# Spreading the root of each head's mean square: a stride-zero stationary and one product per head in place of a wide tile and transposes

## The chip, the core and the metric

The kernel runs on one core of a Trainium2 chip. The metric is the device time of one execution in microseconds (us). TensorE is PE in the profile (its weight loads are listed apart as PEld), VectorE is DVE, ScalarE is ACT, GpSimd is POOL, and SyncE, which issues the DMAs, is SP.

## What is computed

Two layers over 512 latent tokens and 256 context tokens, model width 1024. Layer 0 is grouped-query attention, layer 1 a bidirectional state-space mixer; each is followed by a gated FFN with a short convolution. What matters here is the normalization, which occurs in two shapes:

```python
def rms_norm(x, g):
    xf = x.astype(jnp.float32)
    y = xf * lax.rsqrt(jnp.mean(xf * xf, axis=-1, keepdims=True) + EPS)
    return (y * g.astype(jnp.float32)).astype(x.dtype)
...
    q_l = rms_norm(q_l.reshape(bsz, seq, N_HEADS, HEAD_DIM), q_norm)
    k_l = rms_norm(k_l.reshape(bsz, seq, N_KV_HEADS, HEAD_DIM), k_norm)
...
        h_l = modulate(rms_norm(x, norm_mix_w[i]), mod_l[0], mod_l[1])
```

Before every mixer and FFN the norm runs over the whole width of 1024 (one root per token). On queries and keys it runs per head of 64 (one root per token and head): 16 query heads and 4 key heads, 768 tokens each.

## The kernel before

All activations lie transposed: channels on the 128 partitions, tokens along the free dimension. A tile of queries or keys therefore holds two heads, one on partitions 0 to 63 and one on 64 to 127, and 768 tokens in six groups of 128. There are ten such tiles (eight of queries, two of keys).

The large matrix products run in fp32r, each as three products of a high and a low part (`mm3`, lines 103 to 111). Products whose operands are plain fp32 go through the same instruction. The trace counts how many records an instruction leaves, and this count will matter: a transpose leaves one, an fp32r product one, a plain fp32 product two.

The helper `rstd_rows` (lines 235 to 267) makes the roots. It is a generator in two halves with a `BREAK` between them:

1. Sums of squares. For each group of 128 tokens, the squared tile is the stationary operand and `cols` the moving one (line 244), so that a group's tokens come to lie on partitions and the result has `c` columns: `c` is 1 for the norm over the width and 2 for queries and keys (one column per head). DVE adds epsilon (line 247), ACT takes the logarithm and the exponential (line 249), DVE makes one Newton step (lines 251, 252 and its last multiply).
2. The way back. The root is on the token's partition, but it has to multiply a tile with tokens along the free dimension. So every group is transposed on PE into a PSUM bank, four groups to a bank, and the yielded bank is the second operand of a DVE multiply (line 552 for queries and keys, line 294 for the others).

For `c` = 1 the last Newton multiply writes the small tile `a` (128 x 6 at most) and the transpose reads one of its columns with a stride of zero 128 times. For `c` = 2 the last multiply writes a wide tile `rb` (128 x 768), in which every root stands 64 times (line 259, tile `rbq` in the trace), and the transpose reads 128 columns of it.

Where it is called:

- queries and keys, ten times, in `normed` (line 538), each with two yields of the second half: four groups (512 latent tokens), then two (256 context tokens). The first two calls (keys 0, queries 0) lie in the context projection (`ps_c`, line 719), where the scheduler has put their six transposes together. The next two (queries 1 and 2) lie in the value projection (`ps_v`, line 533). The other six lie in the steps of the head pairs, one in each of the first six pairs (line 789), where PE runs the scores (`ps_s`, line 697), the maxima (`ps_m`, line 625), the value products (`ps_o`, `ps_oc`, line 661), the sums (`ps_sum`, line 667) and pieces of the query projection (`ps_q`) in the order of the program. There the transposes follow right behind a group of `ps_o`.
- the width norm, six tiles of 128 tokens before attention (`rsTa`), ten in the two FFN norms (`rsTf`), six before the state-space layer (`rsTs`) and four at its gated norm (`rsTy`).

Up to line 515, the first projection, PE, ACT and DVE are ordered by hand; behind that a list scheduler orders instructions by the program's order and its own costs, so a changed instruction can move its neighbours. Tiles named `t3` come from a pool of 18 buffers in this stage; `rb` takes one of them.

Of the kernel before, what the change touches and what calls it, by code (L numbers as in the profile page):

```python
# [7 lines left out]
P = 128  # L8
# [3 lines left out]
ALU = mybir.AluOpType  # L12
# [55 lines left out]
def t3(g, name, dt=F32, n=T):  # L68
    return g.t3p.tile([P, n], dt, tag="t3", bufs=g.n3, name=name)
# [148 lines left out]
def follow(g, bi):  # L218

    if g.last_act is not None:  # L220
        g.tc.add_manual_dep(bi.ins, g.last_act.ins.name, mybir.DependencyInfo(
            mybir.DependencyClass.NoSync, mybir.DependencyReason.DATA), reason="order of tables")
    g.last_act = bi
# [11 lines left out]
def rstd_rows(g, sq, n, cols, width, name, bank):  # L235

    nc = g.nc
    c = cols.shape[-1]  # L240
    nt = n // P
    ps = bank(f"ss{name}")
    for t in range(nt):
        nc.tensor.matmul(ps[:, t * c : (t + 1) * c], sq[:, t * P : (t + 1) * P], cols, start=True, stop=True)
    small = lambda nm: g.p.tile([P, nt * c], F32, tag="rst", bufs=8, name=nm)
    a, y, u = small("rsa"), small("rsy"), small("rsu")
    nc.vector.tensor_scalar(a, ps[:, : nt * c], 1.0 / width, EPS, ALU.mult, ALU.add)

    for f in ((lambda: nc.scalar.activation(y, a, AF.Ln)), (lambda: nc.scalar.activation(y, y, AF.Exp, scale=-0.5))):
        follow(g, f()) if g.tables else f()  # L250
    nc.vector.tensor_tensor(u, y, a, ALU.mult)
    nc.vector.scalar_tensor_tensor(u, y, -0.5, u, ALU.mult, ALU.mult)
    if c == 1:
        nc.vector.scalar_tensor_tensor(a, u, 1.5, y, ALU.add, ALU.mult)
        root = lambda t: a[:, t : t + 1].broadcast_to([P, P])
    else:
        rb = t3(g, f"rb{name}", n=n)
        wide = lambda v: v.unsqueeze(2).broadcast_to([P, nt * c, P // c])
        nc.vector.scalar_tensor_tensor(rb.rearrange("p (a b) -> p a b", b=P // c), wide(u), 1.5, wide(y),
                                       ALU.add, ALU.mult)  # L260
        root = lambda t: rb[:, t * P : (t + 1) * P]
    yield BREAK
    for t0 in range(0, nt, 4):
        pt = bank(f"rsT{name}")
        for t in range(t0, min(nt, t0 + 4)):
            nc.tensor.transpose(pt[:, (t - t0) * P : (t - t0 + 1) * P], root(t), g.ident)
        yield (pt, t0 * P, min(n, (t0 + 4) * P))


# [53 lines left out]
class Norm:  # L323
# [23 lines left out]
    def gen(self, seg, x, lag=2):  # L347

        i, a, b = seg
        g, nc, n = self.g, self.g.nc, b - a  # L350
        for _ in range(lag):
            yield
        rows = rstd_rows(g, self.acc[seg, 6], n, g.ones[:, :1], D, self.name, lambda nm: Bank(g, nm))
        next(rows)
        for _ in range(lag):
            yield
        rs = next(rows)[0][:, :n]
        for m in range(KT):
            modulated(g, self.h[i][m], x[i], rs, a, b, *self.a, self.streams[i][1], m,
                      pool=m in ((1, 4) if a else (1, 3, 5, 7)))  # L360
            yield
# [30 lines left out]
def attention(g, fill, X, late):  # L392
# [57 lines left out]
    for m in range(KT):  # L450
        sq = t2("sql") if m else acc
        nc.scalar.activation(sq, xs[0][m], AF.Square)
        if m:
            nc.vector.tensor_tensor(acc, acc, sq, ALU.add)
    norm = rstd_rows(g, acc, L, g.ones[:, :1], D, "a", Bk)
    g.qn8 = g.const.tile([P, 1], F32, name="qn8")
    nc.vector.tensor_scalar(g.qn8, g.par[:, PC["qn"] : PC["qn"] + 1], HD ** -0.5, None, ALU.mult)
# [23 lines left out]
    for m in range(KT):  # L481
# [11 lines left out]
        if m == 3:  # L493
            norm = rstd_rows(g, sqc, C, g.ones[:, :1], D, "a", Bk)
            next(norm)
# [1034 lines left out]
```

## Time and profile before

| | |
|---|---|
| median of 3 runs | 1875.17 us (1874.18 to 1875.43) |
| profiled execution: its own time | 1875.38 us |
| profiled execution: span | 1873.6 us |
| mean granted PE clock | 0.998 |
| PE busy | 1848.9 us, 99% |
| DVE busy | 1303.6 us, 70% |
| ACT busy | 807.3 us, 43% |
| POOL busy | 299.8 us, 16% |

The time of an execution is 1.8 us above its span. A timeline row gives the start, the length, the engine, the line, the operation with its tiles (output, then inputs), the shape (stationary rows * columns, then the moving partitions x columns) and a count. A row of several records is merged: its length runs from the first start to the last end, so the spacing of n records of length d in a row of length T is (T - d) / (n - 1). Matmuls are pipelined, and their own lengths overlap; spacing and the start of the next row are what cost time. The bracket at a row's end is idle time of the engine before it and what ended that.

### The profile page before, as it was taken

The numbers are of one execution on the slowest core, as the hardware profiler recorded it, in microseconds if no ns is written. First come the engines' busy times: TensorE is split into PE (matmuls) and PEld (weight loads), VectorE is DVE, ScalarE is ACT, GpSimd is POOL, SyncE is SP. The second block draws the span as 40 slices with busy tenths as digits, with TensorE's granted clock in tenths as the row PEclk, the third lists the DMA queues.
The fourth block names the chain that finished last, engine by engine and source line by source line (L and its number), as shares of the span: only waits on it lengthen the run. The fifth ranks groups of instructions, "written<-read, shape, count | busy, mean of one in ns | idle before, by whom it ended". The sixth has DMA issues, their size and how long they took to land.

```text
span 1873.6 us, 28798 instructions
## 1 busy us (share of the span) xinstructions
PE 1848.9 (99%) x11474; PEld 1547.2 (83%) x11474; DVE 1303.6 (70%) x1950; ACT 807.3 (43%) x1402; POOL 299.8 (16%) x266
## 2 busy tenths in 40 slices
PE   9999999999999999999999999999999999999999
PEld 8876656798888888888888888888887888888887
DVE  6588888778787776544487787777797565565655
ACT  4534444363122222222367667776666352323231
POOL 2123120040000000000032333444443210000000
PEclk9999999999999999999999999999999999999999
DMA  9233151124444552211224432443352223222232
GB/s 345 76 109 101 63 178 52 57 84 164 146 135 145 191 185 99 68 58 56 68 91 141 124 105 87 124 124 113 124 178 93 79 91 97 95 95 97 90 103 89
DMA packets 74070, 211.67 MB, mean 113 GB/s; under 512 B 9040, under 2 KB 14544, under 8 KB 73808
## 3 DMA queue, kind: packets, MB, share of 16 engines
q1 hardware_dynamic: 73936, 209.84, 34.0%
q8 instruction: 90, 1.47, 0.3%
q14 instruction: 44, 0.36, 0.1%
HBM read 198.79 MB, written 6.82 MB: 110 GB/s over the span
## 4 chain that ended last, share of the span: by engine, by line
PE 84%; DVE 7%; issue 3%; DMA 2%; POOL 2%; ACT 2%; SPq 0%; DVEq 0%; POOLq 0%; ACTq 0%
PE ps_up L108 10%; PE ps_up L111 10%; PE ps_up L109 10%; PE ps_d L108 6%; PE ps_d L111 6%; PE ps_d L109 6%; PE ps_in L111 4%; PE ps_in L109 4%; PE ps_in L108 4%; PE ps_s L697 2%; PE ps_o L661 2%; PE ps_st L1123 2%; DMA wada<-in_adaA 1%; PE ps_wo L111 1%; PE ps_wo L108 1%
## 5 line engine op out<-in xcount | busy, mean ns | idle before, releaser
L87 DVE TENSOR_TENSOR wl<-wst,wh 128x1024 fp32r<-128x1024 f32 x207 | 258.5, 1249 | 233.9 <-PE ps_up L109 138.9
L85 ACT CAST wh<-wst 128x1024 fp32r<-128x1024 f32 x211 | 221.3, 1049 | 393.7 <-DMA wst<-in_wup 323.6
L108 PE MATMUL ps_up<-hhf,wh 128*128 128x512 f32 x1008 | 357.6, 355 | 0.0
L109 PE MATMUL ps_up<-hlf,wh 128*128 128x512 f32 x1008 | 357.3, 354 | 0.0
L111 PE MATMUL ps_up<-hhf,wl 128*128 128x512 f32 x1008 | 357.0, 354 | 0.0
L108 PEld LDWEIGHTS ps_up<-hhf,wh 128*128 128x128 f32 x1008 | 190.8, 189 | 26.4
L109 PEld LDWEIGHTS ps_up<-hlf,wh 128*128 128x128 f32 x1008 | 190.8, 189 | 26.3
L111 PEld LDWEIGHTS ps_up<-hhf,wl 128*128 128x128 f32 x1008 | 190.6, 189 | 26.4
L108 PE MATMUL ps_in<-hhs,wh 128*128 128x512 f32 (+1 forms) x560 | 204.4, 365 | 1.5 <-ACT dt L1008 1.5
L109 PE MATMUL ps_in<-hls,wh 128*128 128x512 f32 (+1 forms) x560 | 199.4, 356 | 0.0
L111 PE MATMUL ps_in<-hhs,wl 128*128 128x512 f32 (+1 forms) x560 | 198.7, 355 | 0.0
L108 PE MATMUL ps_d<-hdh,wh 128*128 128x512 f32 (+1 forms) x568 | 193.3, 342 | 0.2 <-ACT hdh L85 0.2
L111 PE MATMUL ps_d<-hdh,wl 128*128 128x512 f32 (+1 forms) x568 | 193.5, 341 | 0.0
L109 PE MATMUL ps_d<-hdl,wh 128*128 128x512 f32 (+1 forms) x568 | 192.9, 340 | 0.3 <-DVE hdl L87 0.3
L874 DVE SCALAR_TENSOR_TENSOR X<-ps_d,mod,X 128x512 f32<-128x512 f32 (+1 forms) x224 | 124.3, 583 | 35.9 <-PE ps_d L111 35.2
L108 PEld LDWEIGHTS ps_in<-hhs,wh 128*128 128x128 f32 x560 | 105.9, 189 | 16.6 <-ACT dt L1008 1.7
L109 PEld LDWEIGHTS ps_d<-hdl,wh 128*128 128x128 f32 x568 | 106.7, 188 | 14.8 <-DVE hdl L87 0.7
L111 PEld LDWEIGHTS ps_in<-hhs,wl 128*128 128x128 f32 x560 | 105.8, 189 | 14.7
L111 PEld LDWEIGHTS ps_d<-hdh,wl 128*128 128x128 f32 x568 | 106.6, 188 | 13.1
L108 PEld LDWEIGHTS ps_d<-hdh,wh 128*128 128x128 f32 x568 | 106.3, 188 | 13.4 <-ACT hdh L85 0.7
L109 PEld LDWEIGHTS ps_in<-hls,wh 128*128 128x128 f32 x560 | 106.0, 189 | 13.2
L700 ACT ACTIVATE pr<-ps_s 128x1024 f32<-128x1024 f32 x56 | 57.2, 1021 | 107.2 <-PE ps_s L699 107.2
(339 smaller groups left out, 3653.4 us busy)
## 6 DMA issues: line engine op xcount, KB each, us to landing
wst<-in_wup SPq DMA_DIRECT2D x88, 512.0 KB, 3.3
wada<-in_adaT SPq DMA_DIRECT2D x56, 512.0 KB, 3.3
wst<-in_win SPq DMA_DIRECT2D x48, 512.0 KB, 3.4
wst<-in_wdown SPq DMA_DIRECT2D x44, 512.0 KB, 3.5
E<-ad SPq DMA_DIRECT2D x64, 256.0 KB, 6.9
wada<-in_adaB SPq DMA_DIRECT2D x24, 512.0 KB, 4.1
ec<-ead SPq DMA_DIRECT2D x64, 128.0 KB, 5.6
wst<-in_wout SPq DMA_DIRECT2D x16, 512.0 KB, 3.3
```

Source lines behind the costliest of these rows:

```text
L85: cast = keep(nc.scalar.copy(hi, src))
L87: keep(eng.tensor_tensor(lo, src, _r(hi), ALU.subtract))
L108: mm(out, wh, ah, start=first, stop=False)
L109: mm(out, wh, al, start=False, stop=False)
L111: mm(out, wl, ah, start=False, stop=last)
L661: nc.tensor.matmul(po[S64[e], :n], v, pr[:, 512 * e + off : 512 * e + off + n], start=first, stop=last)
L697: nc.tensor.matmul(outs[e], kk[e][a][S64[e], k], b[S64[e], q], start=i == 0, stop=False)
L700: exps.append(nc.scalar.activation(pr, ps, AF.Exp))
L874: nc.vector.scalar_tensor_tensor(ap, o[:, c0:c1], gate[:, m, v : v + 1], ap, ALU.mult, ALU.add)
L1123: nc.tensor.matmul(ps[:, d * 256 : (d + 1) * 256], Bt[:, t * P : (t + 1) * P], xw[d][t], start=t == ts[0], stop=t == ts[-1])
```

## The change

In `rstd_rows` the branch on `c` goes. The last Newton multiply always writes the small tile `a` (128 x 12 for queries and keys in place of 128 x 768), `rb` is neither allocated nor written, and the transposes of line 266 become fp32 products with the unit matrix as the moving operand (line 260 of the changed kernel). The stationary operand is one column of `a` read with a stride of zero: 64 times for queries and keys, 128 times for the width norm. For queries and keys there are two products for each group of 128 tokens, one per head, which write PSUM partitions 0 to 63 and 64 to 127. For the width norm there is one product where there was one transpose.

```diff
@@ -250,20 +250,15 @@
-    if c == 1:
-        nc.vector.scalar_tensor_tensor(a, u, 1.5, y, ALU.add, ALU.mult)
-        root = lambda t: a[:, t : t + 1].broadcast_to([P, P])
-    else:
-        rb = t3(g, f"rb{name}", n=n)
-        wide = lambda v: v.unsqueeze(2).broadcast_to([P, nt * c, P // c])
-        nc.vector.scalar_tensor_tensor(rb.rearrange("p (a b) -> p a b", b=P // c), wide(u), 1.5, wide(y),
-                                       ALU.add, ALU.mult)
-        root = lambda t: rb[:, t * P : (t + 1) * P]
+    nc.vector.scalar_tensor_tensor(a, u, 1.5, y, ALU.add, ALU.mult)
+    w = P // c
     yield BREAK
     for t0 in range(0, nt, 4):
         pt = bank(f"rsT{name}")
         for t in range(t0, min(nt, t0 + 4)):
-            nc.tensor.transpose(pt[:, (t - t0) * P : (t - t0 + 1) * P], root(t), g.ident)
+            for j in range(c):
+                nc.tensor.matmul(pt[j * w : j * w + w, (t - t0) * P : (t - t0 + 1) * P],
+                                 a[:, t * c + j : t * c + j + 1].broadcast_to([P, w]), g.ident, start=True, stop=True)
         yield (pt, t0 * P, min(n, (t0 + 4) * P))
```

On PE the place of the instructions stays and their number grows. This is PE at the first call, inside the context projection; `rsTq` is the bank of roots, `rbq` the wide tile, `rsa` the small one, and the first of the two shapes is the output's.

```order
 L109 MATMUL ps_c<-hla_7_133,wsh 128x256
 L111 MATMUL ps_c<-hha_7_132,wsl 128x256
-L266 MATMUL rsTq<-cst,rbq 128x128 x6
+L260 MATMUL rsTq<-cst,rsa 64x128 x12
 L108 MATMUL ps_c<-hha_0_118,wsh 128x256
 L109 MATMUL ps_c<-hla_0_119,wsh 128x256
```

Six transposes became twelve products of half the width, between the same neighbours.

On DVE the scheduler puts some neighbours of the removed write in another order. These are DVE's rows around the write of `rbq` for queries 0, before the change; `raw_896` is the tile of keys 0, `raw_897` that of queries 0, `kl` the low part of the keys.

```order
L251 TENSOR_TENSOR rsu<-rsy,rsa 128x12
L548 TENSOR_TENSOR raw_896<-raw_896,qsw 128x512
L252 SCALAR_TENSOR_TENSOR rsu<-rsy,rsu 128x12
L259 SCALAR_TENSOR_TENSOR rbq<-rsu,rsy 128x768
L552 TENSOR_TENSOR raw_896<-raw_896,rsTq 128x512
L552 TENSOR_TENSOR raw_896<-raw_896,rsTq 128x256
L87 TENSOR_TENSOR wl<-wst,wh 128x1024
L87 TENSOR_TENSOR kl_1138<-raw_896,kh_1137 128x768
```

And the same place with the change:

```order
L253 SCALAR_TENSOR_TENSOR rsa<-rsu,rsy 128x12
L541 TENSOR_TENSOR raw_896<-raw_896,cs 128x512
L542 TENSOR_TENSOR qsw<-qsw,cs 128x512
L543 TENSOR_TENSOR raw_896<-raw_896,qsw 128x512
L547 TENSOR_TENSOR raw_896<-raw_896,rsTq 128x512
L87 TENSOR_TENSOR wl<-wst,wh 128x1024
L547 TENSOR_TENSOR raw_896<-raw_896,rsTq 128x256
L541 TENSOR_TENSOR raw_897<-raw_897,cs 128x512
```

The root of queries 0 is now made ahead of the rotation of keys 0 (lines 541 to 543), and the second multiply of keys 0 stands behind a weight split instead of ahead of it. On SP one load of modulation weights (`wada`, line 125) moves ahead of the copies of the first keys (`khs`, line 564).

## The prediction

> **What bounds the kernel now.** I read the page first, for the engine that sets the end, then PE's waits, then the timeline at the places where the roots are spread.
>
> ```profile
> span 1873.6 us, 28798 instructions
> PE 1848.9 (99%) x11474; PEld 1547.2 (83%) x11474; DVE 1303.6 (70%) x1950; ACT 807.3 (43%) x1402; POOL 299.8 (16%) x266
> PE 84%; DVE 7%; issue 3%; DMA 2%; POOL 2%; ACT 2%; SPq 0%; DVEq 0%; POOLq 0%; ACTq 0%
> ```
>
> PE is busy for 99% of the span and carries 84% of the chain that ended last. DVE has 7%. Time taken from DVE is worth something only where PE stands and waits; time given to PE costs its full length except there. Next, the stages that hold queries and keys (stretch, then for each engine its busy time), and who PE waits for in them:
>
> ```profile
> 85.00:110.00 25.00, 24.83 (x194) 22.25 (x194) 19.31 (x28) 11.28 (x20) 7.72 (x7) 1.00 0.36 110
> 110.00:280.00 170.00, 167.20 (x1355) 102.78 (x1353) 139.39 (x197) 72.82 (x101) 39.28 (x22) 1.00 0.34 115
> ...
> PE ps_s L697 <- ACT pr L700: 1.8, 2, 1.4
> PE ps_s L699 <- DVE diag L648: 1.4, 2, 0.7
> PE ps_m L625 <- DVE ma L627: 1.3, 1, 1.3
> ```
>
> DVE is loaded there (139.39 of 170 us), but PE is not waiting: from 75 to 380 us its waits sum to 1.8 + 1.4 + 1.3 = 4.5 us. That is the whole cover in this stretch, and the most that a faster DVE could give.
>
> **What goes from DVE.** The two forms of the last Newton multiply (count, then least, median and greatest duration in ns):
>
> ```profile
> L254 DVE SCALAR_TENSOR_TENSOR rsa<-rsu,rsy x11: 160/161/163, 14.7 to 1509.9; 128x2 f32<-128x2 f32 x9, 128x4 f32<-128x4 f32 x2
> L259 DVE SCALAR_TENSOR_TENSOR rbq<-rsu,rsy x10: 957/958/1634, 73.3 to 262.2; 128x768 f32<-128x768 f32 x10
> ...
> PEld rsTq L266 <- DVE rbq L259: 0.2, 1, 0.2
> ```
>
> Ten times 958 - 161 ns is 8.0 us of DVE. PE's weight load waits for the wide write in one call only, for 0.2 us; I count 0.2 us as gained. The other rows that carry less than DVE's wait lie in the rivals.
>
> **What PE does now for queries and keys.** First the group in the context projection, six transposes; then one of the six calls behind `ps_o`, four and two; then the pass from `ps_o` to `ps_sum`, which keeps the shape:
>
> ```profile
> 78.28 0.28 PE L111 MATMUL ps_c<-hha,wsl 128*128 128x256 f32 x1
> 78.39 0.82 PE L266 MATMUL rsTq<-cst,rbq 128*128 128x128 f32 x6
> 78.96 0.37 PE L108 MATMUL ps_c<-hha,wsh 128*128 128x256 f32 x1
> ...
> 124.68 1.08 PE L661 MATMUL ps_o<-pr,v 128*64 128x512 f32 x4
> 125.69 0.66 PE L266 MATMUL rsTq<-cst,rbq 128*128 128x128 f32 x4
> 126.10 0.36 PE L108 MATMUL ps_q<-hha,wh 128*128 128x256 f32 x1
> 128.69 1.08 PE L661 MATMUL ps_o<-pr,v 128*64 128x512 f32 x4
> 129.70 0.44 PE L266 MATMUL rsTq<-cst,rbq 128*128 128x128 f32 x2
> 129.90 0.36 PE L108 MATMUL ps_q<-hha,wh 128*128 128x256 f32 x1
> ...
> 136.44 1.08 PE L661 MATMUL ps_o<-pr,v 128*64 128x512 f32 x4
> 137.35 1.03 PE L667 MATMUL ps_sum<-acc,ones 128*64 128x512 f32 x4
> ```
>
> From a group's first start to the next row's: 0.57 us for six transposes (78.39 to 78.96), 0.41 for four, 0.20 for two; the spacing inside is (0.82 - 0.27) / 5 = 0.11. The four `ps_o` records hold PE for 1.01 us ahead of transposes (124.68 to 125.69) but 0.91 us ahead of `ps_sum`: leaving the shape 128*64 costs 0.10.
>
> **What PE will do.** The trace holds an almost exact copy of the new group: `ps_y`, plain fp32, stationary 128*64, moving 128x128, in pairs that write partitions 0 to 63 and 64 to 127.
>
> ```profile
> L1197 PE MATMUL ps_y<-E,xt x256: 272/273/323, 1043.5 to 1425.8; 128*64 128x128 f32 x128
> ...
> 1042.76 0.83 PE L1188 MATMUL ps_yo<-Cf,hs 128*128 128x128 f32 x6
> 1043.52 1.09 PE L1197 MATMUL ps_y<-E,xt 128*64 128x128 f32 x16
> 1044.55 0.50 PE L108 MATMUL ps_in<-hhs,wh 128*128 128x512 f32 x1
> ```
>
> The code issues 128 such products (8 groups x 2 pairs x 4 chunks x 2 heads) and the row counts 256 records: two per product. Their spacing is (1.09 - 0.273) / 15 = 0.0545 us. Sixteen take 0.87, and the next row starts 1.03 after the first, so leaving the group costs 0.16. Entering it: the last `ps_yo` starts at 1042.76 + 0.83 - 0.275 = 1043.32, 0.20 before the group, where 0.11 is its usual spacing: 0.09 for entry. I take these three prices; the weight is read at stride zero here and not in `ps_y`, but the stride-zero transposes of the width norm (below) load no slower than the others.
>
> A group over n tiles has 4n records and lasts 4n x 0.0545 + 0.16: 1.47 us for six, 1.03 for four, 0.60 for two. Against the transposes that is +0.90, +0.62 and +0.40. Then:
>
> - context projection: entry 0.09 is new, 2 x (0.90 + 0.09) = 1.98 us;
> - value projection, groups of four and two: 2 x (0.62 + 0.09 + 0.40 + 0.09) = 2.40 us;
> - the five calls behind `ps_o` in pairs 0 to 4: the shape is kept, so 0.10 falls away at each group, 5 x (0.52 + 0.30) = 4.10 us;
> - the sixth, in pair 5, is followed by the one long wait:
>
> ```profile
> 276.20 1.08 PE L661 MATMUL ps_o<-pr,v 128*64 128x512 f32 x4
> 278.71 0.38 PE L697 MATMUL ps_s<-qh,kh 64*128 64x256 f32 x1 [1.43 <-ACT pr L700]
> ```
>
> Its 0.82 us fit into 1.43, whose end is set by POOL's rotation of the queries, the DVE behind it and the ACT cast; without this cover it would cost 0.82. The waits for `diag` and `ma` I do not count as cover: DVE works there on maxima that PE delivers shortly before, so they move with PE. For the same reason I put the new order in the context projection at nothing, on DVE (one weight split ahead of keys 0) and on SP (one load of `wada` ahead of the copies of the first keys):
>
> ```profile
> L87 DVE TENSOR_TENSOR wl<-wst,wh 128x1024 fp32r<-128x1024 f32 x207 | 258.5, 1249 | 233.9 <-PE ps_up L109 138.9
> ...
> 78.40 0.53 SPq L125 DMA_DIRECT2D wada<-in_adaB  x1
> 80.95 1.15 SPq L564 DMA_DIRECT2D khs<-kh  x2
> ```
>
> SP stands idle between those two issues, longer than one more of 0.53 us takes, and PE runs on `ps_c` and `ps_v` meanwhile, while the maxima that need the first keys and queries move back by the same 1.98 us. Without this cover it is at most the split, 1.2 us.
>
> Queries and keys: 1.98 + 2.40 + 4.10 - 0.2 = 8.3 us.
>
> Where the Trainium skill would have it otherwise: "TensorE: Matmul & The Clock Gate", Part 3, says that matmuls whose outputs lie in different column groups run concurrently in the array. By that the two heads of a tile would share one spacing and the sum would lose half its records, 10 x 12 x 0.0545 = 6.5 us. The rows do not bear it out: see the first rival.
>
> **What PE pays for the width norm.** Per tile one transpose becomes two records with a stationary of 128 columns, which is `ps_yo`'s shape:
>
> ```profile
> 1050.12 1.95 PE L1188 MATMUL ps_yo<-Cf,hs 128*128 128x128 f32 x16
> ...
> L266 PE MATMUL rsTf<-cst,rsa x10: 270/272/323, 382.1 to 1510.2; 128*128 128x128 f32 x10
> L266 PE MATMUL rsTs<-cst,rsa x6: 270/272/323, 938.2 to 962.9; 128*128 128x128 f32 x6
> L266 PE MATMUL rsTy<-cst,rsa x4: 270/272/273, 1466.7 to 1467.0; 128*128 128x128 f32 x4
> ...
> L266 PEld LDWEIGHTS rsTs<-cst,rsa x6: 132/134/136, 938.2 to 962.8; 128*128 128x128 f32 x6
> L266 PEld LDWEIGHTS rsTq<-cst,rbq x60: 137/141/144, 78.3 to 274.5; 128*128 128x128 f32 x60
> ...
> 19.02 0.63 PE L132 MATMUL ps_ada<-wada,sc 128*32 128x64 f32 x16 [1.80 <-DMA wada<-in_adaA]
> ```
>
> (1.95 - 0.275) / 15 = 0.112 us per record, so 2 x 0.112 - 0.11 = 0.114 more per tile. For 20 tiles (10 + 6 + 4) that is 2.3 us, wherever they lie: in PE's stream, or ahead of a multiply that PE waits for. The six tiles before attention I put at nothing: the first projection waits for its weights (1.80 us for `wada` at 19.02); without that cover they cost 0.7.
>
> **Sum.** 8.3 + 2.3 = 10.6 us. The profiled execution took 1875.38 us, 0.21 above the median; I add the sum to the median, 1875.17 + 10.6 = 1885.8 us.
>
> **The rivals.**
>
> 1. *The column halves overlap*, the page's rule. The sum falls by 6.5 us to 4.1: 1879.3 us. Against it: `ps_o` and `ps_sum` above are also pairs on two column halves, and four records hold PE for 0.91 us, 0.23 each; at a quarter of that moving size `ps_y` shows 0.0545, about a quarter. Spacing follows what each record streams, not pairs. Chance 0.06.
> 2. *The shape costs more at each of the 16 groups.* Nearest row above: a single record's length, 0.27 us, if the array emptied fully on entry and again on exit. The groups in the trace show 0.09 and 0.16, so 2 x 0.27 - 0.25 = 0.29 more, 16 x 0.29 = 4.7: 1890.5 us. Against it: `ps_y` passes through the same shapes. Chance 0.10.
> 3. *DVE was the pace-setter in the query stages* (the other side). DVE is 82% busy from 110 to 280 us, and it loses 8.0 us. If PE's steps were waiting for it in small pieces that the wait view books as issue, PE's additions for queries and keys would vanish in those pieces, and 8.0 - 2.3 = 5.7 us would be gained: 1869.5 us. It decides once such waits exceed the 8.3 us added. Booked waits are 4.5, and PE is busy 167.2 of 170, so all its idle time there is 2.8 us. Chance 0.04, half of it for a partial effect that ends near no change.
>
> **How the numbers follow.** My forecast has the remaining 0.80, and 1885.8 us is its value. Range: at the low end entry and exit cost nothing (-3.1) and DVE closes the 3.1 us of waits not yet counted, 10.6 - 6.2 = 4.4, which the first rival reaches too; I set 1880.0. At the high end stands the second rival, 1890.5. About 0.2% (3.75 us) can be told from no change: faster means below 1871.4, slower above 1878.9. Forecast and rivals 1 and 2 all lie above, 0.96 with a little taken off for the first, which is close to the border: slower 0.94, within 0.2% 0.04, faster 0.02.
>
> **What would show it.** In the changed profile, `rsTq` has 240 PE records of shape 128*64 at 0.054 to 0.056 us spacing (0.027 on average for the first rival), a six-tile group lasts about 1.47 us to the next row, `rsTf`, `rsTs` and `rsTy` have twice their records, L259's wide write is gone and DVE's busy time is some 8 us less, PE's about 10 us more, and the 1.43 us wait in pair 5 is shorter by about 0.8. Wrong would be: records of `rsTq` at 120 in place of 240, a PE wait on DVE that disappears along with its length, or new PE waits above 1 us in the attention stage.

## The result and the profile after

The kernel after takes 1883.34 us (median of 5 runs, 1882.76 to 1884.79), the kernel before 1875.17 (1873.35 to 1876.10) on the same chip: a ratio of 1.0046, 95% interval 1.0031 to 1.0061. The change makes the kernel slower by 8.2 us, where 10.6 was forecast. The profiled execution of after took 1883.34 us.

The page of after, the same three lines as of before:

```profile
span 1881.5 us, 29215 instructions
PE 1858.3 (99%) x11680; PEld 1556.3 (83%) x11680; DVE 1293.9 (69%) x1950; ACT 807.2 (43%) x1402; POOL 299.5 (16%) x266
PE 81%; DVE 9%; issue 4%; ACT 2%; POOL 2%; DMA 1%; SPq 0%; POOLq 0%; DVEq 0%; ACTq 0%
```

PE has 206 records more and 9.4 us more of busy time; DVE has 9.7 us less. The span grew by 7.9: most of what PE gained in work came out as time, what DVE lost did not. The stages of queries and keys (stretch, then the busy time of each engine), and who PE waits for from 75 to 380 us:

```profile
85.00:110.00 25.00, 25.00 (x214) 21.60 (x213) 14.08 (x23) 9.63 (x18) 7.54 (x6) 1.00 0.34 101
110.00:280.00 170.00, 169.29 (x1449) 108.88 (x1449) 130.09 (x195) 72.15 (x102) 38.99 (x22) 1.00 0.33 110
...
PE ps_s L692 <- ACT pr L695: 1.9, 2, 1.5
PE ps_m L620 <- DVE ma L622: 1.3, 1, 1.3
PE ps_s L694 <- DVE diag L643: 0.7, 1, 0.7
```

Of the three waits of before, two stand as they were. The one for `diag` has lost one of its two places and 0.7 us. The new records, by form, and the groups in the context projection and behind `ps_o`:

```profile
L260 PE MATMUL rsTq<-cst,rsa x240: 272/273/323, 78.0 to 280.9; 128*64 128x128 f32 x120
...
L260 PE MATMUL rsTf<-cst,rsa x20: 270/275/376, 388.4 to 1519.0; 128*128 128x128 f32 x20
L260 PE MATMUL rsTs<-cst,rsa x12: 275/275/376, 945.5 to 970.2; 128*128 128x128 f32 x12
L260 PE MATMUL rsTy<-cst,rsa x8: 270/275/275, 1474.4 to 1475.2; 128*128 128x128 f32 x8
...
77.83 0.28 PE L111 MATMUL ps_c<-hha,wsl 128*128 128x256 f32 x1
78.04 1.53 PE L260 MATMUL rsTq<-cst,rsa 128*64 128x128 f32 x24
79.50 0.38 PE L108 MATMUL ps_c<-hha,wsh 128*128 128x256 f32 x1
...
127.36 1.08 PE L656 MATMUL ps_o<-pr,v 128*64 128x512 f32 x4
128.27 1.04 PE L260 MATMUL rsTq<-cst,rsa 128*64 128x128 f32 x16
129.24 0.39 PE L108 MATMUL ps_q<-hha,wh 128*128 128x256 f32 x1
...
132.78 0.61 PE L260 MATMUL rsTq<-cst,rsa 128*64 128x128 f32 x8
133.31 0.39 PE L108 MATMUL ps_q<-hha,wh 128*128 128x256 f32 x1
```

Six tiles last 1.46 us to the next row (79.50 - 78.04, 1.47 forecast), with (1.53 - 0.273) / 23 = 0.0547 us per record. Four tiles behind `ps_o` last 0.97 (1.03 forecast) and two 0.53 (0.60 forecast).

A ledger of the profiled 7.9 us follows from the starts of the same PE record in the two timelines:

| record | before | after | offset | step | forecast |
|---|---|---|---|---|---|
| `ps_c` ahead of the first roots | 78.28 | 77.83 | -0.45 | -0.45 | 0 |
| `ps_c` behind the second call | 82.36 | 83.88 | +1.52 | +1.97 | 1.98 - 0.2 |
| first `ps_s`, behind the value projection | 111.20 | 114.80 | +3.60 | +2.08 | 2.40 |
| `ps_m` behind the first `diag` | 113.16 | 115.83 | +2.67 | -0.93 | 0 |
| `ps_s` at the start of pair 5 | 262.57 | 268.47 | +5.90 | +3.23 | 4.10 |
| `ps_s` behind the long wait in pair 5 | 278.71 | 285.05 | +6.34 | +0.44 | 0 |
| `ps_first`, behind the first FFN's norm | 406.84 | 413.92 | +7.08 | +0.74 | |
| `ps_wo`, behind the state-space norm | 1407.53 | 1415.32 | +7.79 | +0.71 | |
| `ps_wo`, behind the norm of the mixer's output | 1467.02 | 1475.22 | +8.20 | +0.41 | |
| `ps_first`, behind the second FFN's norm | 1511.63 | 1520.43 | +8.80 | +0.60 | 2.3 for these four |
| `ps_first`, 6 us later | 1517.28 | 1525.18 | +7.90 | -0.90 | 0 |

From there to the end the offset stays. Two steps are not put down to the change. The first, -0.45, lies ahead of the roots of queries and keys; in a second pair of profiles (further below) the offset there is +0.30. The last, -0.90, comes from a stretch in which the clock was halved in the execution of before that was profiled, and not in that of after (shown further below). So a ledger of two single executions carries 1 us of chance or more. Without these two the steps come to 9.25 us. The medians are the measure of the whole, but 8.2 us has 5.8 to 11.4 as its bounds, and they too can hold such stretches: the mean granted clock was 1.00 in four of the five runs of after, and in 4 of the 39 runs of before that were made beside the experiments (on three chips).

### The profile page after: what moved, and what is told of

It reads as the page before. It is cut to its first block, busy times and chain, and to the rows that moved or that the text cites. A ratio compares the mean times of both kernels' runs of the same rounds, so it can differ in the third digit from the quotient of the medians.

```text
span 1881.5 us, 29215 instructions
## 1 busy us (share of the span) xinstructions
PE 1858.3 (99%) x11680; PEld 1556.3 (83%) x11680; DVE 1293.9 (69%) x1950; ACT 807.2 (43%) x1402; POOL 299.5 (16%) x266
## 4 chain that ended last, share of the span: by engine, by line
PE 81%; DVE 9%; issue 4%; ACT 2%; POOL 2%; DMA 1%; SPq 0%; POOLq 0%; DVEq 0%; ACTq 0%
PE ps_up L109 10%; PE ps_up L111 10%; PE ps_up L108 10%; PE ps_d L108 6%; PE ps_d L111 6%; PE ps_d L109 6%; PE ps_in L109 4%; PE ps_in L111 4%; PE ps_in L108 4%; PE ps_s L692 2%; PE ps_o L656 2%; PE ps_st L1118 1%; DVE Bf L1048 1%; DVE xf L1048 1%; PE ps_wo L111 1%
```

## The experiments

The question was first which part of the change costs what, then whether the halves of the array overlap, then what took the `diag` wait away.

**Heads only.** Products for queries and keys, transposes for the width norm as before.

```diff
+            if c == 1:
+                nc.tensor.transpose(pt[:, (t - t0) * P : (t - t0 + 1) * P], a[:, t : t + 1].broadcast_to([P, P]), g.ident)
+                continue
             for j in range(c):
```

> Queries and keys by stride-zero products, the width norm by its transposes as before. Theory: the cost is TensorE's, call by call. In the trace of the changed kernel the offset against before grows by 1.96 us in the two calls of the context projection, 2.05 in the two of the value projection, 3.59 in the six of the pairs, and 0.80 is given back where the wait for diag goes: 6.8 us, so about 1882 us. If the width norm carried what the prediction gave it (2.3 us), 1881. Rival, VectorE sets the pace in the query stages and the growth comes from elsewhere: below 1877 us.

1880.60 us (1879.53 to 1881.64), 1.0028 of before with 1.0017 to 1.0039; before took 1875.44 in these runs. So the heads cost 5.2 us, with 3.2 to 7.3 as bounds. That is less than the 6.8 us which I had read from the ledger (1882), and close to the 1881 that I gave for a width norm at its forecast price.

**Width only.** The other part by itself: products for `c` = 1, the wide tile and its transposes for `c` = 2.

```diff
-    nc.vector.scalar_tensor_tensor(a, u, 1.5, y, ALU.add, ALU.mult)
+    if c == 1:
+        nc.vector.scalar_tensor_tensor(a, u, 1.5, y, ALU.add, ALU.mult)
+    else:
+        rb = t3(g, f"rb{name}", n=n)
+        wide = lambda v: v.unsqueeze(2).broadcast_to([P, nt * c, P // c])
+        nc.vector.scalar_tensor_tensor(rb.rearrange("p (a b) -> p a b", b=P // c), wide(u), 1.5, wide(y),
+                                       ALU.add, ALU.mult)
...
+            if c == 2:
+                nc.tensor.transpose(pt[:, (t - t0) * P : (t - t0 + 1) * P], rb[:, t * P : (t + 1) * P], g.ident)
+                continue
             for j in range(c):
```

> The width norm by products, queries and keys by the wide tile and transposes as before. Theory: at most 2.3 us (20 tiles at 0.114), and less where a wait behind the product shrinks by as much: between 1.0 and 2.3 us, 1876.2 to 1877.5 us. The 0.66 us wait for diag in the first pair is there as before, since the wide write is. Rival: the width norm costs nothing that can be measured (under 0.5 us), and the whole change is queries and keys.

1877.22 us (1875.65 to 1878.68, 11 runs), 1.0009 of before with 1.0000 to 1.0017: 1.8 us, where 2.3 was forecast. The parts sum to 7.0 against 8.2 for the whole; the intervals cover the gap, so no interaction is shown.

**Wide kept.** The kernel after, and DVE also writes the wide tile of roots, which nobody reads.

```diff
     nc.vector.scalar_tensor_tensor(a, u, 1.5, y, ALU.add, ALU.mult)
     w = P // c
+    if c == 2:
+        rb = t3(g, f"rb{name}", n=n)
+        wide = lambda v: v.unsqueeze(2).broadcast_to([P, nt * c, P // c])
+        nc.vector.scalar_tensor_tensor(rb.rearrange("p (a b) -> p a b", b=P // c), wide(u), 1.5, wide(y),
+                                       ALU.add, ALU.mult)
```

> The changed kernel, and the wide tile is written as well, but nobody reads it (ten writes of 0.96 us on VectorE that lead nowhere). Theory: VectorE's time does not set the pace, so the time stays within 1 us of the changed kernel, 1883 to 1884.5 us, and the only place that can show it is the wait for diag in the first pair: if the relief of VectorE removed it, it comes back with 0.5 us or more. Rival, VectorE's 8.0 us are worth their length: 1888 to 1891 us.

1884.35 us (1882.34 to 1885.56), 1.0048 of before with 1.0036 to 1.0061: 1.0 us over after, inside the spread. The write is there (the group of DVE's wide multiplies in this kernel):

```profile
L258 DVE SCALAR_TENSOR_TENSOR rbq<-rsu,rsy 128x768 f32<-128x768 f32 x10 | 9.5, 950 | 0.0
```

Giving back the 9.5 us of DVE costs 1.0 us by the medians, which cannot be told from nothing. The 1888 to 1891 us of the rival lie outside the interval (up to 1886.9), so DVE was not the pace-setter. The surprise is that the wait for the first `diag` does not come back with DVE's work; that is taken up below.

**Heads twice.** Every head product is issued twice.

```diff
             for j in range(c):
-                nc.tensor.matmul(pt[j * w : j * w + w, (t - t0) * P : (t - t0 + 1) * P],
-                                 a[:, t * c + j : t * c + j + 1].broadcast_to([P, w]), g.ident, start=True, stop=True)
+                for _ in range(c):
+                    nc.tensor.matmul(pt[j * w : j * w + w, (t - t0) * P : (t - t0 + 1) * P],
+                                     a[:, t * c + j : t * c + j + 1].broadcast_to([P, w]), g.ident, start=True, stop=True)
```

> Every head product is issued twice (240 records more on TensorE, the same result). Theory: a record costs 0.0545 us, the two column halves do not overlap: 240 x 0.0545 = 13.1 us more than the changed kernel, 1896 us, less at most 1.4 us that the long wait of pair 5 can hide. Rival, the column halves overlap: half of it, 1890 us.

1896.97 us (1896.22 to 1898.18), 1.0117 of before with 1.0103 to 1.0131: 13.6 us over after for 240 more records, 0.057 each. The six-tile group of 48 records (the timeline):

```profile
77.66 2.89 PE L261 MATMUL rsTq<-cst,rsa 128*64 128x128 f32 x48
80.48 0.38 PE L108 MATMUL ps_c<-hha,wsh 128*128 128x256 f32 x1
```

I took this for proof that the halves do not overlap. It proves only that 0.0545 us is the mean price of one more record in this mix; it doesn't say whether that is the price of one alone or half the price of two side by side.

**Halves in blocks.** The records of a bank in another order: all products of head 0, then all of head 1.

```diff
-        for t in range(t0, min(nt, t0 + 4)):
-            for j in range(c):
+        for j in range(c):
+            for t in range(t0, min(nt, t0 + 4)):
                 nc.tensor.matmul(pt[j * w : j * w + w, (t - t0) * P : (t - t0 + 1) * P],
                                  a[:, t * c + j : t * c + j + 1].broadcast_to([P, w]), g.ident, start=True, stop=True)
```

> The kernel after, with the products of a bank in another order: first all of the one head (columns 0 to 63 of the array), then all of the other, in place of one head and the other in turn. If records on the two column halves overlapped at all in the kernel after, blocks of one half would lose it: up to 120 x 0.0545 = 6.5 us more than after, 1890. If they do not, as the doubled products showed (13.6 us for 240 records), the spacing stays at 0.0545 us and the time is that of after within 0.5 us, 1883.3 to 1884. Lower than after would mean that the change of half costs something at each record.

1888.57 us (1887.94 to 1889.13), 1.0073 of before with 1.0059 to 1.0086: 5.2 us over after, for the same records in another order. My theory fell. The timelines show it, first that of after and then that of this kernel, each with the records that start in the first 0.03 us of the group and then the whole of it:

```profile
78.04 0.33 PE L260 MATMUL rsTq<-cst,rsa 128*64 128x128 f32 x2
...
78.04 1.53 PE L260 MATMUL rsTq<-cst,rsa 128*64 128x128 f32 x24
79.50 0.38 PE L108 MATMUL ps_c<-hha,wsh 128*128 128x256 f32 x1
```

```profile
78.04 0.32 PE L260 MATMUL rsTq<-cst,rsa 128*64 128x128 f32 x1
...
78.04 2.02 PE L260 MATMUL rsTq<-cst,rsa 128*64 128x128 f32 x24
79.99 0.38 PE L108 MATMUL ps_c<-hha,wsh 128*128 128x256 f32 x1
```

In after two records stand at 78.04, one for each half; here there is one. The single records behind it show the rest. In after they start in pairs 0.007 us apart, and from the second on one pair follows another by 0.109 us. Here the first records of a block follow each other at 0.109 us, one at a time, and only beside the fifth does another start. So a record holds its half for 0.109 us, and two on different halves run side by side. The group takes 1.95 us in place of 1.46.

**One half.** To take the overlap by itself: the products of the second head are left out, so that half of the roots is missing, and DVE fills that half of the bank with ones.

```diff
+        if c == 2:
+            nc.vector.memset(pt[w:, : min(nt - t0, 4) * P], 1.0)
         for t in range(t0, min(nt, t0 + 4)):
-            for j in range(c):
+            for j in range(1):
```

> The kernel after, with the products of the second head of each query or key tile left out: only columns 0 to 63 of the array are used, 120 records in place of 240, and DVE fills the other half of the bank with ones beforehand (16 to 20 short writes more on DVE, which has room). New theory, after the run with the halves in blocks: a record of 128 columns of moving data holds its half of the array for 0.109 us, and two records on different halves run side by side, which is the 0.0545 us of mean spacing in the kernel after. By it leaving out one half saves next to nothing: six tiles still last about 12 x 0.109 + 0.16 = 1.47 us to the next row, and the time stays within about 1.5 us of after (1882 to 1885 us; the ones may shift a few steps). Rival, each record costs 0.0545 us by itself, as the prediction priced it: six tiles last 12 x 0.0545 + 0.16 = 0.81 us and 120 records save 6.5 us, 1876.8 us.

1887.18 us (1885.37 to 1888.31), 1.0061 of before with 1.0044 to 1.0078; before took 1876.56 in these runs. With half of the records gone the time is no lower than after's, where the rival asked for 1876.8; it is above the 1882 to 1885 that I expected. The six-tile group in the context projection and two groups in pair 0:

```profile
77.94 1.52 PE L262 MATMUL rsTq<-cst,rsa 128*64 128x128 f32 x12
79.39 0.39 PE L108 MATMUL ps_c<-hha,wsh 128*128 128x256 f32 x1
...
129.73 1.04 PE L262 MATMUL rsTq<-cst,rsa 128*64 128x128 f32 x8
130.70 0.39 PE L108 MATMUL ps_q<-hha,wh 128*128 128x256 f32 x1
...
134.22 0.60 PE L262 MATMUL rsTq<-cst,rsa 128*64 128x128 f32 x4
134.75 0.39 PE L108 MATMUL ps_q<-hha,wh 128*128 128x256 f32 x1
```

Twelve, eight and four records last 1.45, 0.97 and 0.53 us: what 24, 16 and 8 last in after (1.46, 0.97, 0.53). The second head is free. That the whole is above after, by 2.4 us (10.6 over before, against 8.2) or 3.8 by the medians, is more than the 1.5 I allowed. The ones bring waits of their own (PE waits 0.76 us for them at 83.16 us) and other places for the groups; I did not take this apart.

**Split on DVE.** The kernel before, with the low part of the first pair's query weights (pair 4) taken on DVE, not on POOL.

```diff
-        cast = split(g, st, *w, lo_engine="pool")
+        cast = split(g, st, *w, lo_engine="dve" if p == 4 else "pool")
```

> The kernel before, with one edit: the low part of the first pair's query weights (pair 4) is taken on DVE, not on POOL, where DVE's order puts it right behind the two multiplies that write diag. Theory: in the kernel before the second of those multiplies (2.75 us, the first 0.56) is held up by POOL's 2.50 us subtract, which reads two operands at the same time, and PE's 0.66 us wait for diag at 112.8 us follows from that; the change removed this wait by moving POOL's subtract 3.6 us later. By it both multiplies take 0.55 to 0.56 us here, PE does not wait for diag at 112 us, and the kernel is up to 0.8 us faster than before (1874.4 to 1875.2 us); the 1.25 us on DVE fall into the 0.84 us in which DVE waits for PE at 113.6, so some 0.4 us of the gain may be lost again. Rival, DVE's own work before diag sets the wait (eight operations stand back to back from 103.9 us on): the second multiply still ends near 112.8 us, the wait stays at 0.6 to 0.7 us and the time is that of before or a little above it (1875.2 to 1876).

1873.43 us (1872.75 to 1874.17, 11 runs), 0.9992 of before with 0.9983 to 1.0001, so 1.9 us less, which cannot quite be told from no change and is more than the 0.8 us that I allowed. The runs at a mean granted clock of 1.00 differ by less: 1872.75 to 1874.13 (four), and 1874.01 and 1874.09 for before. The profile decides more. DVE's two multiplies that write the first `diag` (count, then least, median and greatest duration in ns), with POOL's row at that time where it has one; first before, then after, then the split on DVE:

```profile
L648 DVE TENSOR_TENSOR diag<-id,mz x2: 558/1652/2746, 109.5 to 110.0; 128x384 fp32r<-128x384 f32 x2
...
109.85 2.50 POOL L87 TENSOR_TENSOR wl<-wst,wh 128x1024 fp32r<-128x1024 f32 x1 [9.29 <-PE ps_v L533]
```

```profile
L643 DVE TENSOR_TENSOR diag<-id,mz x2: 553/556/558, 112.1 to 112.5; 128x384 fp32r<-128x384 f32 x2
...
113.45 2.40 POOL L87 TENSOR_TENSOR wl<-wst,wh 128x1024 fp32r<-128x1024 f32 x1 [13.23 <-PE ps_v L528]
```

```profile
L648 DVE TENSOR_TENSOR diag<-id,mz x2: 549/553/557, 108.3 to 108.8; 128x384 fp32r<-128x384 f32 x2
```

In before the second multiply takes 2.75 us and ends at 110.0 + 2.75 = 112.8, 0.4 behind POOL's subtract (109.85 + 2.50): it was held until that was done. With the subtract gone it takes 0.56, and PE's wait for `diag` at 112 us is no longer listed. In after the subtract, released by PE, starts 3.6 us later, behind both multiplies. Width only, where the subtract stays in place, has 2.75 us again; wide kept and heads only, where it moves, have 0.56 us at most. So it is POOL's subtract and not DVE's own load. The Trainium skill, "SBUF — State Buffer", section "SBUF: two separate sides", says that DVE and GpSimd share a pair of ports under an exclusive lock, and that a DVE operation with two SBUF inputs blocks fully against a GpSimd one that reads SBUF. The rows agree: 0.56 us grows by 2.2, most of POOL's 2.5.

**Both kernels profiled again.** No edit.

> The kernel before, unchanged, profiled once more, to see which stretches of the first profile belong to the kernel and which to one execution. If the 0.88 and 1.11 us waits near 1511 us with the granted clock at 0.50 behind them belong to the kernel, they stand here too; if the clock's fall belongs to the execution, the spacing of the f32r records there is 0.23 us and the 1.11 us wait is shorter or gone. The diag multiplies must take 0.56 and 2.75 us again by the theory of POOL's subtract.

> The kernel after, unchanged, profiled once more. Its offset against the other profiles of before and after at the same instruction shows how far one profile's ledger can be trusted: I expect the steps of the query groups (1.96 us in the context projection, 2.0 in the value projection, 3.2 in pairs 0 to 4) again within 0.1 us each, diag without a wait, and differences of up to 1 us only at waits of PE of over 1 us, where the clock may or may not fall.

The spans are 1873.6 and 1882.1 us (1873.6 and 1881.5 before). In this second pair the offset is +0.30 ahead of the first roots and +2.26 behind the second call, a step of 1.96 as expected. The value projection gives 2.30, 0.3 more than expected, and the first `diag` -0.92; in the second profile of before DVE's two multiplies for it take 0.56 and 2.75 us again. Pairs 0 to 4 give 1.65 in place of 3.2, because the stretch with the halved clock moved there: between the two profiles of before the offset goes from -0.60 at 113 us to +1.00 behind the stretch, so it cost 1.6 there. With that added the steps from the first roots to the second FFN's norm come to 10.0 us, against 9.25 in the first pair. At single places the two profiles of after drift by up to 0.6 us (pair 5's wait is 1.7 in place of 1.5). The waits of 0.88 and 1.11 us near 1511 us stand in both profiles of before, so they belong to the kernel, and the fall of the clock behind them to one execution. By windows (the granted clock is the third number from the end), first the first profile of before behind 1511 us, then its second at the same place and at 114 us:

```profile
1511.00:1513.00 2.00, 1.37 (x5) 1.19 (x6) 2.00 (x7) 1.93 (x4) 0.00 (x0) 0.74 0.00 0
1513.00:1515.00 2.00, 2.00 (x10) 1.81 (x9) 2.00 (x6) 2.00 (x6) 0.73 (x1) 0.50 0.00 0
1515.00:1517.00 2.00, 2.00 (x15) 1.87 (x15) 1.69 (x4) 0.94 (x3) 0.88 (x1) 0.91 0.00 0
```

```profile
1513.00:1515.00 2.00, 1.92 (x13) 1.33 (x11) 2.00 (x6) 2.00 (x5) 0.74 (x1) 1.00 0.00 0
...
114.00:116.00 2.00, 2.00 (x48) 1.99 (x51) 1.76 (x5) 0.43 (x2) 1.92 (x3) 0.75 1.04 381
116.00:118.00 2.00, 2.00 (x32) 1.52 (x25) 1.93 (x3) 0.00 (x0) 0.72 (x1) 0.50 0.97 385
118.00:120.00 2.00, 2.00 (x14) 0.84 (x10) 0.90 (x2) 0.97 (x1) 0.00 (x0) 0.89 1.05 395
```

## Why the prediction was right, and where its steps failed

**The direction and the bound held.** PE's records cost their length, DVE's relief bought nothing that could be measured, and most stages of the ledger come out near the working. `rsTq` has 240 records at 0.0547 us, the width norm has doubled its records, and DVE has lost the wide writes. DVE lost 9.7 us where 8.0 was forecast; the multiply for `diag` alone is 2.2 us shorter.

**What sets the price, and what I had wrong about it.** The duration from the `ps_y` row was the right one, since `ps_y` writes the two halves in turn as well. But the sentence against the first rival, "Spacing follows what each record streams, not pairs", is false. A record takes 0.109 us on its half, and 0.0545 is that price halved by the overlap. The rival halved a price that held the overlap already; with 0.109 as the price of one record, the page's rule gives my own sum. So the overlap to which I gave a chance of 0.06 is what happens, while the time that I gave it, 1879.3 us, does not follow from it. That my sum held was luck in this point: the row that I copied held the overlap, and I didn't know it. The Trainium skill, "TensorE: Matmul & The Clock Gate", Part 3, had it right: matmuls on different column tiles run concurrently, and the records start 0.007 us apart here. I used the `ps_o` rows against it, but they are pairs on two halves themselves, four records in 0.91 us, and no row of one half alone stood beside them. So what the change really pays is the second record of a plain fp32 product: per tile two times 0.109 us in place of one transpose at 0.11. Whether it is made of two heads or of one width makes no difference: 0.0545 x 4 = 0.218 for two heads, 2 x 0.112 = 0.224 for one width.

**The groups behind `ps_o`** were the mis-sized term: 4.10 forecast, 3.23 measured. I took the exit from the `ps_y` group as 0.16 us. Here 0.97 - 16 x 0.0545 = 0.10, so that 0.06 falls away ten times. More lies in the transposes of before: I took 0.41 us for four from one place, but where another shape follows they already pay an exit. In pair 1 of before four last 0.58 (156.13 - 155.55), another 0.17, and the remaining 0.1 stays open. In pair 5 four last 0.58 too (270.24 - 269.66):

```profile
155.55 0.66 PE L266 MATMUL rsTq<-cst,rbq 128*128 128x128 f32 x4
156.13 0.50 PE L697 MATMUL ps_s<-qh,kh 64*128 64x512 f32 x1
...
269.66 0.66 PE L266 MATMUL rsTq<-cst,rbq 128*128 128x128 f32 x4
270.24 0.97 PE L132 MATMUL ps_ada<-wada,sc 128*32 128x128 f32 x28
```

The value projection's 2.08 against 2.40 has the same sign; I did not split it further. The context projection, where six transposes were read in place, came out at 1.97 for 1.98, with the 0.2 us of the awaited wide write not to be seen.

**The wait for `diag`** was the step that failed: "The waits for `diag` and `ma` I do not count as cover: DVE works there on maxima that PE delivers shortly before, so they move with PE." For `ma` that holds (1.3 us in both). The first `diag` was late because of POOL, whose subtract is released by the last of the value projection and so moved by 3.6 us, while DVE's multiplies moved by 2.5; they no longer meet. Ledger: -0.93 us (-0.92 in the second pair), a gain that no term had. A wait of PE on DVE that goes with its length was on my own list of signs of being wrong. It did go, but not because DVE had less to do: with the wide writes put back (wide kept) both multiplies still take 0.56 us at most.

**The wait in pair 5** was to swallow 0.82 us and to become shorter. It is 1.49 us, not 0.6:

```profile
285.05 0.38 PE L692 MATMUL ps_s<-qh,kh 64*128 64x256 f32 x1 [1.49 <-ACT pr L695]
```

PE's own work ahead of it grew by only 0.38 (from +5.90 to 285.05 - 1.49 - 278.71 + 1.43 = +6.28), since the transposes of before already paid their exits there, and the chain behind the wait ended 0.44 later than PE's offset at the start of the pair. The cover exists all the same. In heads twice, where the two groups of that call last 1.4 us longer, the wait shrinks to 0.26:

```profile
297.61 0.38 PE L693 MATMUL ps_s<-qh,kh 64*128 64x256 f32 x1 [0.26 <-ACT pr L696]
```

What moved the chain's end by 0.44 us stays open: the same wait is 1.2 us in heads only, 1.5 in width only and 1.7 in wide kept, so it varies by that much from profile to profile, with the products in that call or without. POOL's rotation, with which that chain starts, is a place to look: its first multiply starts at 267.15 in before and 274.53 in after, 7.38 later, but its second lasts 2.26 there and 1.26 here. In the second profile of after the second lasts 2.25, and the wait is 1.74.

**The width norm** held: 2.46 in the ledger (0.74 + 0.71 + 0.41 + 0.60) and 1.8 (0 to 3.2) by itself, for 2.3. The six tiles ahead of attention, put at nothing, show no loss that stands out: the offset ahead of the first roots of the heads is -0.45, and +0.30 in the second pair of profiles.

## What to carry to other kernels

Before a price is taken from a row of pairs, ask whether it already holds an overlap; doubling the work doesn't tell, but leaving one of the two out, or parting them in the order, does. Where PE is the bound, a transpose of one record is not to be replaced by a plain fp32 product of two, however much it spares an engine that PE does not wait for. A wait on one engine can be a third engine's doing: look at what else ran during an operation that took several times its usual length.

## What the runs showed of the hardware that was not expected

- Two records on different column halves start 0.007 us apart, but the overlap depends on how far apart they stand in the program. With four records of a half in a row (heads twice) the mean spacing stays near 0.0545 us. With eight (halves in blocks) no record has another beside it until the fifth; I read that other as the first of the second half, since records of one half stand 0.109 us apart. There a group of six tiles takes 1.95 us in place of 1.46.
- The clock was halved for a stretch of 3.4 us in the middle of some executions and not of others, also of the same kernel: by the rows of the second profile of before, (2 x 0.25 + 2 x 0.50 + 2 x 0.11) / 0.50 = 3.4 us. At half the clock this can cost up to half of its length, 1.7 us, where PE is busy throughout (an estimate from these rows); between the two profiles of before 1.6 was seen at 114 us and 1.0 at 1511 us. No wait of PE as long as the stretch precedes it (0.88 and 1.11 us at 1511 us, 0.64 ahead of 114 us). What sets it off stays open. Single profiles of one kernel can differ by 1 to 1.6 us at a place by this alone.
